# Sums of weights loaded into the tiles of x: six of the loads in each second half's pairs leave the ring `avc`

## The chip, the cores and the metric

The kernel runs on one core of a Trainium2 chip. The metric is the device time of one execution in microseconds (us). Before the change it is 2368.85 us, the median of three runs (2365.73, 2368.85 and 2370.08).

## What is computed

The reference is a trunk of two layers over `x` of 256 tokens by 2048 features, in float32. Each layer adds a token mixer (mLSTM in layer 0, HGRN2 in layer 1) and then a gated feed-forward part to `h`; a last RMSNorm closes it. The change touches the feed-forward part and the norms around it:

```python
def conv_glu(hn, w_up, conv_w, conv_b, w_down):
    u = hn @ w_up                                  # 2048 -> 2 x 5504
    a, v = jnp.split(u, 2, axis=-1)
    ...                                            # c: convolution of width 3 over the tokens of a
    return (jax.nn.gelu(c, approximate=False) * v) @ w_down   # 5504 -> 2048
...
    h = h + mix
    h = h + conv_glu(rmsnorm(h, norm_ffn_g[layer]), ...)
return rmsnorm(h, final_g)
```

## The kernel before, in words

**Streaming and splitting.** The weights come from HBM in the order in which PE (the matrix engine) uses them. SP, the engine that issues these DMAs, loads tiles `raw` of 128x2048 floats (`load_raw`, L135; in the up-projection L395), of which three exist. A piece of a `raw` is cast on ACT to a rounded high part `wh` (L147) and DVE subtracts this from the original to get the low part `wl` (L148). A product of two matrices is three matmuls: high by high, high by low, low by high. `x`, the normed input of a projection, is split in the same way into the tiles `xt0` to `xt15`, one for each k-tile of 128 features (`Norm.take`).

**The feed-forward part** of a layer has two halves. The first holds 22 of the 43 k-tiles of the middle dimension and the second 21. In a half the up-projection comes first, one chunk per k-tile, 64 matmuls on the 16 tiles of x (L357 and L361); what it gives goes through bias, convolution, gelu and the split in scratch tiles `avc` (L1195 to L1207) and ends in tiles `g`. Then come two *pairs* (`pair`, run by `squares_by_seven`, whose matmuls are L236): the down-projection from the half's k-tiles to two of the four column blocks of 512 each. Two k-tiles form a *couple* u; couple u with two column blocks is a 2x2 block product. The couples in `SEVEN` need seven products instead of eight, Strassen's way (21 matmuls instead of 24), with sums of activations (`sx`) and four sums of weights: T2 and T3 (128x1024 together), T4 and T1 (128x512 each).

**Where the sums of weights come from.** For the couples in `FLY`, DVE makes them on the spot (`combine`, L207). All others are *stored*: `prepare` makes them during earlier stages and writes them to a scratch `tscr` in DRAM (L635). In the pair, `raw(u)` in `split_squares` then issues three DMAs: the couple's weights without B12 (1536 columns, L135), T2, T3 and T4 in one DMA of 128x1536 into a tile `T` (L198), and T1 into the columns of `raw` that are left (L199). The tile `T` is a buffer of the ring `avc`, of which there are `TEMP` = 3, and which the up-projection's scratch `avc` uses too. So a load L198 waits until DVE and ACT have read the buffer that was filled three turns earlier.

**What sets the order.** The program is written as if it ran one thing after the other. A framework puts the instructions of each engine into an order by simulating the engines, and places a semaphore wait wherever a tile is read, written or used again. Each engine, SP included, works its list off strictly in order: an instruction that waits holds up all behind it. The DMAs of SP share eight semaphores in turn (DMAHW0 to DMAHW7), so that at most eight of them are under way.

**x's tiles.** The second half's last up chunk is the last reader of `xt0` to `xt15`. They stand empty during the two pairs of that half, until the next norm writes them (layer 0: the norm of the HGRN2 mixer, whose transposes are L434) or the final norm puts its gain into four of them (`FinalNorm.load`, tiles `fg`, and two tiles `fl` in `half`).

Of the kernel before, what the change touches and what calls it, by code (L numbers as in the profile page):

```python
# [8 lines left out]
F32 = mybir.dt.float32  # L9
F32R = mybir.dt.float32r  # L10
# [5 lines left out]
P = 128  # L16
T = 256
D = 2048
KT = D // P
# [31 lines left out]
FLY = (2,), (5,), (2,), ()  # L51
FIRST = 6
SPLIT = (0, 2, 5), (0, 2, 5)
END = 3
SCRATCH = 4096
SEVEN_MIX = (2, 4, 6)
# [10 lines left out]
def trunk_kernel(ctx, tc, xT, x_d, fg_d, pp_d, cst_d, w_gate, w_first, w_aq, w_ak, w_av, w_ao, w_aout, w_ao2,  # L67
                 w_bq, w_bv, w_bg, w_bout, w_bo2, w_up, w_d0, w_d1, w_d3, out, mscr, tscr):
    nc = tc.nc
    act, dve, pool, pe = nc.scalar, nc.vector, nc.gpsimd, nc.tensor  # L70

    keep = ctx.enter_context(tc.tile_pool(name="keep", bufs=1))
# [110 lines left out]
    def temporary(pool_, name):  # L183
        ff = pool_.name == "ff"
        return pool_.tile([P, 1536], F32, tag="avc" if ff else name, bufs=TEMP if ff else 2, name=name)

    def split_squares(ch, parts):

        units, raws, kept = (ch.nk + 1) // 2, {}, {}
        side.until(lambda: all(ch.waits))  # L190

        def raw(u):
            if u not in raws and u < units:
                n = 1536 if u in ch.stored else min(2048, 1024 * ch.nk - 2048 * u)
                raws[u] = load_raw(ch.src, 2048 * u, 2048 * u + n)
                if u in ch.stored:
                    kept[u] = temporary(ch.pool, "T")
                    nc.sync.dma_start(kept[u], ch.stored[u][:, 0:1536])  # L198
                    nc.sync.dma_start(raws[u][:, 1536:2048], ch.stored[u][:, 1536:2048])  # L199
            return raws.get(u)  # L200

        def combine(u):
            r, T = raw(u), temporary(ch.pool, "T")
            B11, B22, B21, B12 = (r[:, j * 512:(j + 1) * 512] for j in range(4))
            T2, T3, T4 = (T[:, j * 512:(j + 1) * 512] for j in range(3))
            for x, y, out in ((B12, B22, T3), (B12, B11, B12), (B22, B12, T2), (B21, T2, T4)):
                dve.tensor_tensor(out, x, y, ALU.subtract)  # L207
            kept[u] = T

        for u in range(units):  # L210
            r = raw(u)
            yield *parts(r[:, 0:1024], 1024, more=ch.pool), 1
            if u + 1 in ch.seven and u + 1 not in ch.stored:
                combine(u + 1)
            if u in ch.seven:
                yield *parts(kept[u][:, 0:1024], 1024, more=ch.pool), 1
            if 2 * u + 1 < ch.nk:
                yield *parts(r[:, 1024:2048], 1024, more=ch.pool), 1
            if u in ch.seven:
                yield *parts(kept[u][:, 1024:1536], 512, more=ch.pool), 1  # L220

    def banks():
        return [psm.tile([P, 512], F32, tag="mm", name="mm") for _ in range(2)]
# [1 line left out]
    def squares_by_seven(ch, fetch, ready):  # L225
# [48 lines left out]
        for u in range(units):  # L274
            if ch.last and u == units - END:
                ending(u)
# [121 lines left out]
    class Norm:  # L398

        def __init__(self, gname, goff):  # L400
            self.g, self.o = gname, goff
            self.xs, self.rc_, self.R_ = [None] * KT, None, None

        def take(self, k, src, g=None, *pin):
            self.xs[k] = keep.tile([P, 2 * T], F32R, tag=f"xt{k}", name=f"xt{k}")
            split(self.xs[k], src, col(self.g, self.o + k) if g is None else g, *pin)

        def squares(self, c, pin=lambda ins: ins):
# [67 lines left out]
    class FinalNorm:  # L476
# [4 lines left out]
            self.rc = small[:, 8:10]  # L481

        def load(self):
            self.g = [keep.tile([P, 512], F32, tag=f"xt{c}", name=f"fg{c}") for c in range(4)]
            for c in range(4):
                pool.dma_start(self.g[c], fg_d[:, c * 512:(c + 1) * 512].broadcast_to([P, 512]))

# [17 lines left out]
        def half(self, ps, t):  # L505
            side.drain()
            ss, rc = self.ss[:, t], self.rc[:, t:t + 1]
            dve.tensor_tensor(hm[:, t, 1024:1536], hm[:, t, 1024:1536], ps[0], ALU.add)
            square(hm[:, t, 1024:1536], ss[:, 2:3])
            dve.tensor_scalar(rc, ss[:, 2:3], 1.0 / D, rc, ALU.mult, ALU.add)  # L510
            last = keep.tile([P, 512], F32, tag=f"xt{4 + t}", name="fl")
            h = hm[:, t, 1536:2048]
            dve.tensor_tensor(h, h, ps[1], ALU.add)
            m = 256 if t else 512
            dve.scalar_tensor_tensor(last[:, 0:m], h[:, 0:m], 1.0 / D, h[:, 0:m], ALU.mult, ALU.mult, accum_out=ss[:, 3:4])
            dve.tensor_tensor(rc, rc, ss[:, 3:4], ALU.add)
# [58 lines left out]
    def pair(src, nk, c0, x, sums, norm, seven):  # L575
# [31 lines left out]

        ch = Chunk("st", src, nk, x, done)
        ch.mid, ch.seven, ch.sums = mid, seven, sums
        ch.stored, ch.waits, ch.pool, ch.ends, ch.rest = {}, (), None, False, False  # L610
        return ch

    def prepare(tiles, todo, first, period, finished, start, ahead):
# [561 lines left out]
    def ffn(layer, norm, nxt):  # L1175
# [40 lines left out]
        for part, (f0, nf) in enumerate(((0, FA), (FA, FB))):  # L1216
# [14 lines left out]
                                    fixed=part + i > 0))  # L1231
            def two(src, c0, norm, seven, fly, shares, GT=GT, SX=SX, nf=nf):
                ch = pair(src, nf, c0, lambda k: GT[k], lambda u: SX[u], norm, seven)
                ch.waits, left = [], [u for u in seven if u not in fly]
                for n, (todo, finished) in zip(shares, [early[layer]] + lists):
                    for u in left[:n]:
                        store(ch, src, u, todo)
                    if n:
                        ch.waits.append(finished)
                    left = left[n:]  # L1240
                assert not left
                pairs.append(ch)
                return ch
# [26 lines left out]
    c, close0 = ffn(0, n1, n2)  # L1270
    chunks += c
    c = hgrn(n2, n3)
    b = c[0].before
# [6 lines left out]
    c, close1 = ffn(1, n3, nf)  # L1280
# [102 lines left out]
```

## Time and profile before

| | |
|---|---|
| runs | 2365.73, 2368.85, 2370.08 us |
| the profiled execution, its own time | 2366.48 us |
| its span, first to last instruction | 2364.5 us |
| granted clock of PE | 0.999 |
| layer 0, second half: its first pair starts | 975.12 us |
| layer 1, second half: its first pair starts | 2250.33 us |

The profiled execution is one more run. Its span leaves out 2.0 us around the first and last instruction. PE is busy nearly throughout, so that a gap in its row is what counts; a DMA or another engine matters only where it makes PE wait. Engines are PE, DVE (vector), ACT (scalar), POOL and SP; L numbers are lines of the kernel before.

### The profile page before, as it was taken

Reading aid. Unit: us, or ns where it says so; the run is one execution under the profiler, and the core shown is the slowest. Engines: PE = TensorE matmul, PEld = TensorE weight load, DVE = VectorE, ACT = ScalarE, POOL = GpSimd, SP = SyncE. Lnnn points to the kernel's source line nnn. Section 1 sums busy time; section 2 is a strip of 40 time slices with the busy share of each in tenths; the row PEclk is TensorE's granted clock in tenths of the full one; section 3 lists DMA queues with packets and bytes.
Section 4 is the critical chain, followed back from the end, with each engine's and each line's share of the span. In section 5 each row is a group of like instructions: output and inputs, shape, how many; then the busy total and the mean of one; then the engine's idle time right before and its main releaser. Section 6 shows DMA issues by size and latency. Waiting matters only on the chain. (4 is left out here: it accounts for less than half of the span.)

```text
span 2364.5 us, 38407 instructions
## 1 busy us (share of the span) xinstructions
PE 2354.1 (100%) x14545; PEld 2016.2 (85%) x14545; DVE 1993.5 (84%) x3087; ACT 1470.0 (62%) x2340; POOL 196.5 (8%) x244
## 2 busy tenths in 40 slices
PE   9999999999999999999999999999999999999998
PEld 8888888888888888888888888888888888888887
DVE  7777687888998898897888888778789889888888
ACT  7655456555665555676777777776555567455565
POOL 0100000000000000000232322220000000000000
PEclk9999999999999999999999999999999999999999
DMA  8776656888888878996556665646788888888896
GB/s 303 239 248 242 213 195 211 295 282 292 313 321 327 306 282 292 330 334 230 208 203 223 212 225 204 214 169 228 270 300 289 289 321 335 295 287 302 309 351 221
DMA packets 122266, 632.97 MB, mean 268 GB/s; under 512 B 13776, under 2 KB 14928, under 8 KB 77664
## 3 DMA queue, kind: packets, MB, share of 16 engines
q1 hardware_dynamic: 120384, 626.51, 75.0%
q0 software_dynamic: 1120, 3.21, 0.8%
q8 instruction: 114, 1.87, 0.3%
q10 hardware_dynamic: 576, 0.79, 0.1%
q14 instruction: 72, 0.59, 0.1%
HBM read 562.24 MB, written 68.22 MB: 267 GB/s over the span
## 5 line engine op out<-in xcount | busy, mean ns | idle before, releaser
L357 PE MATMUL mm<-xt,wh 128*128 128x512 f32 x3776 | 1312.0, 394 | 0.0
L148 DVE TENSOR_TENSOR wl<-raw,wh 128x1024 fp32r<-128x1024 f32 (+1 forms) x844 | 1037.3, 1234 | 222.6 <-ACT wh L147 214.5
L147 ACT CAST wh<-raw 128x1024 fp32r<-128x1024 f32 (+1 forms) x844 | 875.3, 1042 | 513.0 <-PE mm L357 305.8
L361 PE MATMUL mm<-xt,wl 128*128 128x256 f32 x3776 | 1043.5, 278 | 0.0
L357 PEld LDWEIGHTS mm<-xt,wh 128*128 128x128 f32 x3776 | 705.6, 188 | 160.6 <-issue 0.4
L361 PEld LDWEIGHTS mm<-xt,wl 128*128 128x128 f32 x3776 | 709.4, 188 | 4.5
L373 PE MATMUL mm<-wh,xt 128*128 128x512 f32 x1024 | 324.4, 392 | 0.6 <-ACT wh L147 0.5
L236 PE MATMUL pc<-wh,g 128*128 128x512 f32 (+1 forms) x716 | 243.2, 388 | 0.3 <-ACT wh L147 0.2
L373 PEld LDWEIGHTS mm<-wh,xt 128*128 128x128 f32 x1024 | 191.2, 188 | 40.0 <-ACT wh L147 1.1
L632 DVE TENSOR_TENSOR praw<-praw 128x512 f32<-128x512 f32 x252 | 174.1, 691 | 44.7 <-DMA praw<-in_w_d 29.0
L373 PE MATMUL mm<-wl,xt 128*128 128x512 f32 x512 | 199.7, 391 | 0.0
L236 PEld LDWEIGHTS pc<-wh,g 128*128 128x128 f32 x716 | 134.1, 188 | 29.0 <-ACT wh L147 1.5
L236 PE MATMUL mm<-wh,sx 128*128 128x512 f32 x432 | 153.4, 389 | 0.0
L148 DVE TENSOR_TENSOR wl<-T,wh 128x1024 fp32r<-128x1024 f32 (+1 forms) x144 | 135.9, 955 | 13.3 <-ACT wh L147 8.9
L147 ACT CAST wh<-T 128x1024 fp32r<-128x1024 f32 (+1 forms) x144 | 118.6, 835 | 44.7 <-DMA T<-tscr 18.2
L236 PE MATMUL pc<-wl,g 128*128 128x512 f32 (+1 forms) x358 | 138.8, 388 | 0.0
L591 POOL TENSOR_TENSOR hm<-hm,u 128x512 f32<-128x512 f32 x10 | 14.8, 1481 | 1223.8 <-DVE u L590 1223.8
L373 PEld LDWEIGHTS mm<-wl,xt 128*128 128x128 f32 x512 | 96.2, 188 | 18.6
L1071 DVE TENSOR_TENSOR QK<-QK,G 128x256 f32<-128x256 f32 x224 | 104.6, 515 | 6.2 <-ACT kq L1050 5.9
L1195 ACT COPY avc<-mm 128x256 f32<-128x256 f32 x172 | 64.0, 372 | 63.9 <-PE mm L361 63.6
L1050 ACT COPY kq<-QK 128x512 f32<-128x512 f32 x112 | 74.5, 669 | 37.3 <-DVE QK L1071 29.5
L236 PEld LDWEIGHTS mm<-wh,sx 128*128 128x128 f32 x432 | 81.0, 188 | 16.9 <-ACT wh L147 0.2
(246 smaller groups left out, 2263.1 us busy)
## 6 DMA issues: line engine op xcount, KB each, us to landing
raw<-in_w_up SPq DMA_DIRECT2D x172, 1024.0 KB, 6.1
tscr<-praw SPq DMA_DIRECT2D x126, 512.0 KB, 6.7
praw<-in_w_d SPq DMA_DIRECT2D x120, 512.0 KB, 6.8
raw<-in_w_bq SPq DMA_DIRECT2D x48, 1024.0 KB, 5.0
T<-tscr SPq DMA_DIRECT2D x63, 768.0 KB, 7.6
raw<-in_w_d SPq DMA_DIRECT2D x60, 768.0 KB, 6.0
raw<-in_w_ao SPq DMA_DIRECT2D x24, 1024.0 KB, 4.8
raw<-in_w_d SPq DMA_DIRECT2D x24, 1024.0 KB, 7.7
```

Source lines behind the costliest of these rows:

```text
L147: pin(act.copy(wh[:, :m], r))
L148: pin(dve.tensor_tensor(wl[:, :m], r, wh[:, :m].bitcast(F32), ALU.subtract))
L236: pin(pe.matmul(ps, a, b, start=bank not in begun, stop=stop and i == 2))
L357: hold(pe.matmul(ps[f], wh[:, c:c + P], x, start=k + kk == 0, stop=False))
L361: hold(pe.matmul(ps[f][:, 0:T], wl[:, c:c + P], x[:, 0:T], start=False, stop=k + kk == ch.nk - 1))
L373: pe.matmul(ps[t], x[:, a + t * P:a + (t + 1) * P], w[:, c], start=st and i == 0, stop=sp and i == 2)
L591: pool.tensor_tensor(part(1, 0), part(1, 0), u, ALU.add)
L632: dve.tensor_tensor(out, x, y, ALU.subtract)
L1050: act.copy(m, blocks(QK, h))
L1071: dve.tensor_tensor(two[:, j], two[:, j], by[:, j], ALU.mult)
L1195: act.copy(z, p[:, T:2 * T])
```

## The change

`LENT` names three couples: 2, 3 and 4. In both pairs of a second half, in both layers, their T2 and T3 go into a whole tile of x (`xt3`, `xt5`, `xt6`) and their T4 into half of another (`xt4`, its other half, and half of `xt7`), instead of into a buffer of the ring `avc`. Since the place is in two tiles, the load is two DMAs, of 128x1024 and 128x512. For this the tiles of x now hold two k-tiles each: `xt0` to `xt7`, 128x1024 (in `before`, sixteen of half that size). The final norm's gain lies in the halves of `xt0` and `xt1`, and its scratch `fl` in the halves of `xt2`. All three couples are stored ones, in both layers.

```diff
+LENT = {2: (3, 4, 0), 3: (5, 4, 1), 4: (6, 7, 0)}
...
     def split_squares(ch, parts):
-        units, raws, kept = (ch.nk + 1) // 2, {}, {}
+        units, raws, kept, halves = (ch.nk + 1) // 2, {}, {}, {}
         side.until(lambda: all(ch.waits))
+
+        def place(u):
+            if u not in ch.lent:
+                T = temporary(ch.pool, "T")
+                return T[:, 0:1024], T[:, 1024:1536], T
+            i, j, h = ch.lent[u]
+            if j not in halves:
+                halves[j] = keep.tile([P, 1024], F32, tag=f"xt{j}", name="T")
+            return keep.tile([P, 1024], F32, tag=f"xt{i}", name="T"), halves[j][:, h * 512:(h + 1) * 512], None
...
                 if u in ch.stored:
-                    kept[u] = temporary(ch.pool, "T")
-                    nc.sync.dma_start(kept[u], ch.stored[u][:, 0:1536])
+                    kept[u] = place(u)
+                    for T, a, b in [(kept[u][2], 0, 1536)] if kept[u][2] else zip(kept[u], (0, 1024), (1024, 1536)):
+                        nc.sync.dma_start(T, ch.stored[u][:, a:b])
                     nc.sync.dma_start(raws[u][:, 1536:2048], ch.stored[u][:, 1536:2048])
...
-                yield *parts(kept[u][:, 0:1024], 1024, more=ch.pool), 1
+                yield *parts(kept[u][0], 1024, more=ch.pool), 1
...
-                yield *parts(kept[u][:, 1024:1536], 512, more=ch.pool), 1
+                yield *parts(kept[u][1], 512, more=ch.pool), 1
...
-            self.xs[k] = keep.tile([P, 2 * T], F32R, tag=f"xt{k}", name=f"xt{k}")
+            if k // 2 not in self.two:
+                self.two[k // 2] = keep.tile([P, 4 * T], F32R, tag=f"xt{k // 2}", name=f"xt{k // 2}")
+            self.xs[k] = self.two[k // 2][:, k % 2 * 2 * T:(k % 2 + 1) * 2 * T]
...
-            self.g = [keep.tile([P, 512], F32, tag=f"xt{c}", name=f"fg{c}") for c in range(4)]
+            g = [keep.tile([P, 1024], F32, tag=f"xt{c}", name=f"fg{c}") for c in range(3)]
+            self.g = [g[c // 2][:, c % 2 * 512:(c % 2 + 1) * 512] for c in range(4)]
+            self.last = g[2]
...
-            last = keep.tile([P, 512], F32, tag=f"xt{4 + t}", name="fl")
+            last = self.last[:, 512 * t:512 * t + 512]
...
                 ch = pair(src, nf, c0, lambda k: GT[k], lambda u: SX[u], norm, seven)
+                if part:
+                    ch.lent = LENT
```

The number of instructions on PE, DVE, ACT and POOL stays the same; SP issues 12 more, three in each of four pairs. Every engine's order and waits are the same in both kernels up to the last up chunks of layer 0's second half, and again from the HGRN2 mixer's first chunk to layer 1's second half. What is between differs.

**SP where layer 1's second half turns to its first pair.** Before: T_23012 is couple 1's T, raw_23107 to raw_23233 the weights of couples 2 to 5, and T_23109, T_23151 and T_23193 the T of couples 2 to 4.

```order
L198 DMA T_23012<-tscr 128x1536 [waits DMAHW7_49]
L135 DMA raw_23107<-in_w_d0 128x1536 [waits DMAHW0_49,DVE_49]
L199 DMA raw_23107<-tscr 128x512 [waits DMAHW1_49]
L135 DMA raw_23149<-in_w_d0 128x1536 [waits DMAHW2_49,DVE_49]
L199 DMA raw_23149<-tscr 128x512 [waits DMAHW3_49]
L135 DMA raw_23191<-in_w_d0 128x1536 [waits DMAHW5_49,DMAHW4_49,DVE_49]
L198 DMA T_23109<-tscr 128x1536 [waits DVE_49]
L199 DMA raw_23191<-tscr 128x512 [waits DMAHW6_49]
L198 DMA T_23151<-tscr 128x1536 [waits DMAHW7_49,DVE_49]
L198 DMA T_23193<-tscr 128x1536 [waits DMAHW0_49,DVE_49]
L135 DMA raw_23233<-in_w_d0 128x1536 [waits DMAHW1_49,DVE_49]
```

The changed kernel at the same place: T_22990 is couple 1's T; raw_23084, raw_23128 and raw_23171 are the weights of couples 2 to 4; T_23087 and T_23086 hold the two parts of couple 2's sums, and so on. The lines L209 and L210 are L198 and L199 of before.

```order
L209 DMA T_22990<-tscr 128x1536 [waits DMAHW5_49]
L136 DMA raw_23084<-in_w_d0 128x1536 [waits DMAHW6_49,DVE_49]
L210 DMA raw_23084<-tscr 128x512 [waits DMAHW7_49]
L209 DMA T_23087<-tscr 128x1024 [waits DMAHW0_49,PE_49]
L136 DMA raw_23128<-in_w_d0 128x1536 [waits DMAHW1_49,DVE_49]
L210 DMA raw_23128<-tscr 128x512 [waits DMAHW2_49]
L209 DMA T_23086<-tscr 128x512 [waits DMAHW3_49,PE_49]
L209 DMA T_23086<-tscr 128x512 [waits DMAHW4_49]
L209 DMA T_23130<-tscr 128x1024 [waits DMAHW5_49,PE_49]
L209 DMA T_23174<-tscr 128x1024 [waits DMAHW6_49,PE_49]
L209 DMA T_23173<-tscr 128x512 [waits DMAHW7_49,PE_49]
L136 DMA raw_23171<-in_w_d0 128x1536 [waits DMAHW0_49,DVE_49]
```

Couple 2's T2 and T3 now stand ahead of couple 3's weights, where they stood behind couple 4's, and wait for PE's last reading of a tile of x instead of for DVE. All six lent loads stand ahead of couple 4's weights.

**SP further on in the same pair.** Before: raw_23275, raw_23317 and raw_23359 are the weights of couples 6, 7 and 8, T_23235, T_23277 and T_23319 the T of couples 5 to 7, and T_23470 is the T of the second pair's couple 1.

```order
L135 DMA raw_23233<-in_w_d0 128x1536 [waits DMAHW1_49,DVE_49]
L199 DMA raw_23233<-tscr 128x512 [waits DMAHW2_49]
L198 DMA T_23235<-tscr 128x1536 [waits DMAHW5_49,DMAHW3_49,DVE_49]
L135 DMA raw_23275<-in_w_d0 128x1536 [waits DMAHW4_49,DVE_49]
L199 DMA raw_23275<-tscr 128x512
L198 DMA T_23277<-tscr 128x1536 [waits DMAHW7_49,DMAHW6_49,DVE_49]
L135 DMA raw_23317<-in_w_d0 128x1536 [waits DVE_49]
L199 DMA raw_23317<-tscr 128x512 [waits DMAHW0_49]
L198 DMA T_23319<-tscr 128x1536 [waits DMAHW1_49,DVE_49]
L135 DMA raw_23359<-in_w_d0 128x2048 [waits DMAHW2_49,DVE_49]
```

The changed kernel: raw_23215, raw_23257 and raw_23299 are the weights of couples 5, 6 and 7; T_23217, T_23259 and T_23301 are the T of couples 5 to 7; T_23537, T_23582 and T_23536 belong to couples 2 and 3 of the *second* pair.

```order
L209 DMA T_23217<-tscr 128x1536 [waits DMAHW2_49,DVE_49]
L209 DMA T_23259<-tscr 128x1536 [waits DMAHW3_49,DVE_49]
L209 DMA T_23537<-tscr 128x1024 [waits DMAHW4_49,DVE_49]
L136 DMA raw_23215<-in_w_d0 128x1536 [waits DMAHW5_49,DVE_49]
L210 DMA raw_23215<-tscr 128x512 [waits DMAHW6_49]
L209 DMA T_23301<-tscr 128x1536 [waits DMAHW7_49,DVE_49]
L209 DMA T_23582<-tscr 128x1024 [waits DMAHW0_49,DVE_49]
L209 DMA T_23536<-tscr 128x512 [waits DMAHW1_49,DVE_49]
L209 DMA T_23536<-tscr 128x512 [waits DMAHW2_49]
L136 DMA raw_23257<-in_w_d0 128x1536 [waits DMAHW3_49,DVE_49]
L210 DMA raw_23257<-tscr 128x512 [waits DMAHW4_49]
```

The second pair's lent loads are issued during the first pair, as soon as DVE has read the first pair's sums out of the tiles of x, and ahead of the first pair's couple 6. So are T6 (ahead of couple 5's weights) and T7 (ahead of couple 6's).

**ACT at couple 2 of the same pair.** Before: wh_23097 is from couple 1's T4; wh_23112 and wh_23132 are from couple 2's weights and wh_23122 from its T2 and T3; L1200 and L1203 belong to the last up chunk's convolution and gelu.

```order
L147 CAST wh_23097<-T_23012 128x512
L1195 COPY avc_23035<-mm_22931 128x256
L1200 ACTIVATE avc_23035<-avc_23035,pp_70 128x256
L1203 ACTIVATE avc_23035<-avc_23035 128x256
L147 CAST wh_23112<-raw_23107 128x1024
L1206 CAST g20_23046<-avc_23035 128x256
L147 CAST wh_23122<-T_23109 128x1024
L147 CAST wh_23132<-raw_23107 128x1024
```

The changed kernel, where wh_23101 is from couple 2's T2 and T3, and wh_23091 and wh_23111 from its weights (L1215 and L1218 are L1200 and L1203 of before).

```order
L148 CAST wh_23074<-T_22990 128x512
L1210 COPY avc_23013<-mm_22909 128x256
L1215 ACTIVATE avc_23013<-avc_23013,pp_70 128x256
L148 CAST wh_23101<-T_23087 128x1024
L1218 ACTIVATE avc_23013<-avc_23013 128x256
L148 CAST wh_23091<-raw_23084 128x1024
L148 CAST wh_23111<-raw_23084 128x1024
L1221 CAST g20_23024<-avc_23013 128x256
```

The cast of T2 and T3 has moved from behind the cast of the couple's weights to ahead of the gelu. On PE two matmuls with `wh` of T2 and T3 now come first in couple 2, ahead of the first two with the couple's weights; before, the couple's weights came first with all six of their matmuls.

More of the change, by code (lines that the diff above doesn't have):

```diff
@@ L202, in combine @@
         def combine(u):
-            r, T = raw(u), temporary(ch.pool, "T")
+            r, (T, T4, _) = raw(u), place(u)
             B11, B22, B21, B12 = (r[:, j * 512:(j + 1) * 512] for j in range(4))
-            T2, T3, T4 = (T[:, j * 512:(j + 1) * 512] for j in range(3))
+            T2, T3 = (T[:, j * 512:(j + 1) * 512] for j in range(2))
             for x, y, out in ((B12, B22, T3), (B12, B11, B12), (B22, B12, T2), (B21, T2, T4)):
                 dve.tensor_tensor(out, x, y, ALU.subtract)
-            kept[u] = T
+            kept[u] = T, T4
         for u in range(units):
@@ L401, in __init__ @@
             self.g, self.o = gname, goff
-            self.xs, self.rc_, self.R_ = [None] * KT, None, None
+            self.xs, self.two, self.rc_, self.R_ = [None] * KT, {}, None, None
         def take(self, k, src, g=None, *pin):
-            self.xs[k] = keep.tile([P, 2 * T], F32R, tag=f"xt{k}", name=f"xt{k}")
+            if k // 2 not in self.two:
+                self.two[k // 2] = keep.tile([P, 4 * T], F32R, tag=f"xt{k // 2}", name=f"xt{k // 2}")
+            self.xs[k] = self.two[k // 2][:, k % 2 * 2 * T:(k % 2 + 1) * 2 * T]
             split(self.xs[k], src, col(self.g, self.o + k) if g is None else g, *pin)
@@ L609, in pair @@
         ch.mid, ch.seven, ch.sums = mid, seven, sums
-        ch.stored, ch.waits, ch.pool, ch.ends, ch.rest = {}, (), None, False, False
+        ch.stored, ch.waits, ch.pool, ch.ends, ch.rest, ch.lent = {}, (), None, False, False, {}
         return ch
```

## The prediction

> **What bounds the kernel now.** I read the page's busy row first, then what PE waits for, then the PE row at each place that the change touches, and behind it ACT, DVE and the landings of the DMAs there.
>
> ```profile
> PE 2354.1 (100%) x14545; PEld 2016.2 (85%) x14545; DVE 1993.5 (84%) x3087; ACT 1470.0 (62%) x2340; POOL 196.5 (8%) x244
> ```
>
> PE is busy 2354.1 of 2364.5 us, and the change leaves its instructions as they are. So the sum is about gaps in PE's row, and there are few. The waits of PE, in all, the number of times and the longest, in us:
>
> ```profile
> PE idle L1266 <- POOL ones L1259: 1.1, 1, 1.1
> PE mm L236 <- DVE wl L148: 0.5, 1, 0.5
> PE mm L373 <- ACT wh L147: 0.5, 2, 0.3
> PE pc L236 <- ACT wh L147: 0.2, 1, 0.2
> ```
>
> The first row is the start of the program, the third the start of HGRN2 (L373 is its first product). Both waits of the pairs (L236) lie in layer 1's second half, in its first pair. PE's row there (start, duration):
>
> ```profile
> 2250.33 0.40 PE L236 MATMUL pc<-wh,g 128*128 128x512 f32 x1
> ...
> 2260.31 0.39 PE L236 MATMUL pc<-wh,g 128*128 128x512 f32 x1
> 2260.54 0.49 PE L236 MATMUL mm<-wh,g 128*128 128x512 f32 x1
> 2260.86 0.40 PE L236 MATMUL pc<-wh,g 128*128 128x512 f32 x1
> 2261.79 0.50 PE L236 MATMUL mm<-wl,g 128*128 128x512 f32 x1 [0.53 <-DVE wl L148]
> 2262.13 0.40 PE L236 MATMUL mm<-wh,g 128*128 128x512 f32 x1
> ...
> 2263.39 0.50 PE L236 MATMUL pc<-wh,g 128*128 128x512 f32 x1
> 2263.73 0.39 PE L236 MATMUL mm<-wh,sx 128*128 128x512 f32 x1
> ```
>
> From the pair's first matmul (2250.33) to couple 2's first (2260.54) lie couple 0's 24 matmuls and couple 1's 21: 10.21 / 45 = 0.227 us each, the undisturbed pace. From 2260.31 to 2263.73 PE takes ten steps, which would be 2.27 us, and needs 3.42. **The stall at couple 2 costs 1.15 us**, in three gaps. Its causes stand on ACT, and behind ACT on a DMA:
>
> ```profile
> 2259.12 0.42 ACT L1203 ACTIVATE avc<-avc 128x256 f32<-128x256 f32 x1 [1.13 <-DVE avc L1202]
> 2259.44 1.03 ACT L147 CAST wh<-raw 128x1024 fp32r<-128x1024 f32 x1
> ...
> 2261.34 1.05 ACT L147 CAST wh<-T 128x1024 fp32r<-128x1024 f32 x1 [0.56 <-DMA T<-tscr]
> ```
>
> The cast of couple 2's weights stands behind the last gelu, for which ACT sat idle 1.13 us, and ends at 2260.47, just when PE wants it; DVE's subtraction behind it is what PE waits 0.53 us for. The cast of T2 and T3 then waits 0.56 us for its DMA, and the next cast of weights behind it is the gap at 2263.39. That DMA was issued late, since the ring `avc` was full:
>
> ```profile
> L198 SPq DMA_DIRECT2D T<-tscr x1: 432/432/432, 2255.4 to 2255.4; - x1
> DMA to landing us min/median/max: 5.9/5.9/5.9
> ```
>
> It was issued at 2255.4 and landed at 2261.3.
>
> **The change part by part. 1: the stall at couple 2 goes, −1.1 us.** T2 and T3 now wait for PE's last reading of `xt3` (k-tiles 6 and 7). The last up chunk, and what stands ahead of the load on SP, couple 2's weights:
>
> ```profile
> 2239.00:2250.00 11.00, 11.00 (x66) 9.61 (x65) 9.11 (x14) 6.16 (x10) 2.21 (x4) 1.00 0.96 340
> 2242.16 0.33 SPq L135 DMA_DIRECT2D raw<-in_w_d  x1
> L135 SPq DMA_DIRECT2D raw<-in_w_d x1: 333/333/333, 2247.1 to 2247.1; - x1
> DMA to landing us min/median/max: 9.2/9.2/9.2
> ```
>
> The chunk's matmuls take 11.00 / 66 = 0.167 us, and 32 of its 64 come behind k-tile 7, so this is read 5.3 us before 2250.33, at 2245.0. The load starts ten microseconds earlier than before. By the list it goes out just ahead of couple 3's weights, which landed at 2256.3; with its 0.52 MB more (1.2 us at 0.42 MB per us, part 4) and their 0.79 less (1.9 us) it lands at about 2255.6. Its cast stands ahead of the gelu in ACT's list, where ACT was idle 1.13 us, and takes 1.05: it is hidden there, ends by 2259.1, and gives PE two matmuls (0.45 us) that it now does first. The weights' low part was ready when the matmul at 2261.79 began, and now isn't wanted before 2260.54 plus seven or more steps, 2262.1. So none of the three gaps has a cause left, and what is late next is couple 3's weights, which had no gap. The price if the load landed after 2258 is up to the whole of it: 0 to −1.15, and I take −1.1.
>
> **2: the ring's other loads come earlier,** since three buffers less are asked of it in each pair: T5, T6 and T7 are not late in either kernel (no row of PE waits for them). Nothing.
>
> **3: twelve more DMAs.** A load becomes two. What a DMA of 256 KB costs in a full queue is shown by neighbours, the T1 of couples 3 and 7 (L199) and T7 (L198):
>
> ```profile
> L199 SPq DMA_DIRECT2D raw<-tscr x1: 424/424/424, 2247.5 to 2247.5; - x1
> DMA to landing us min/median/max: 9.5/9.5/9.5
> ...
> L199 SPq DMA_DIRECT2D raw<-tscr x1: 414/414/414, 2273.2 to 2273.2; - x1
> DMA to landing us min/median/max: 7.0/7.0/7.0
> L198 SPq DMA_DIRECT2D T<-tscr x1: 319/319/319, 2274.6 to 2274.6; - x1
> DMA to landing us min/median/max: 7.6/7.6/7.6
> ```
>
> Couple 3's T1 landed at 2257.0, 0.7 us behind its weights (2256.3, above); T7's 0.79 MB landed at 2282.2, 2.0 us behind T1 of couple 7 at 2280.2. That is time by bytes, some 0.4 MB per us, with no visible fixed part: a load cut in two costs the queue nothing. The issue costs SP 0.4 us more, and SP has nothing else to do but wait. I take 0; the upper bound is rival D.
>
> The Trainium skill, "DMA: Bandwidth & Descriptors", speaks against the cut: it wants DMAs of 1 MiB or more, and its section "Anatomy of one DMA — SWDGE (gpsimd) path" fits a DMA's time as 2.0 us and bytes by 436 GB/s. By that, as serial time, 12 more DMAs would be an estimated 24 us; the rows above show no such step between neighbours on this queue, where landings overlap.
>
> **4: arrears in the first pair, +0.5 us.** Now the bytes. Pair two's lent loads are issued in pair one, ahead of couple 6's weights, and so are T6 and T7. DMAs are not idle there:
>
> ```profile
> 2275.00:2280.00 5.00, 5.00 (x24) 4.14 (x23) 4.91 (x6) 4.10 (x5) 0.00 (x0) 1.00 1.02 415
> ...
> 2255.00:2260.00 5.00, 5.00 (x24) 4.14 (x23) 3.71 (x9) 1.48 (x3) 0.00 (x0) 1.00 0.82 291
> 2260.00:2265.00 5.00, 4.47 (x19) 2.93 (x18) 4.14 (x5) 4.44 (x7) 0.00 (x0) 1.00 0.98 354
> 2265.00:2270.00 5.00, 5.00 (x24) 4.14 (x23) 5.00 (x6) 5.00 (x6) 0.00 (x0) 1.00 0.90 317
> ```
>
> The last two columns are the share of the DMA engines and GB/s: full is 1.02 at 0.42 MB per us, and before 2275 some is free. From 2257.0, when couple 3's weights had landed, up to the first 1536 columns of couple 6's weights, the changed list holds 9.17 MB: the six lent loads 2.36, weights of 4, 5 and 6 with two T1 2.88, T5 to T7 2.36, and 1.57 of the second pair's. At 0.42 that lands at 2278.9. Before, it was
>
> ```profile
> L135 SPq DMA_DIRECT2D raw<-in_w_d x1: 333/333/333, 2267.7 to 2267.7; - x1
> DMA to landing us min/median/max: 6.8/6.8/6.8
> ```
>
> 2274.5. PE reaches couple 6 after 24 + 5 x 21 = 129 matmuls, at 2250.33 + 129 x 0.227 = 2279.6; with the cast's 1.05 the weights are ready at 2280.0. So PE is late by 0.4, and I take +0.5. Bounds: nothing, if a part of the lent loads went out before 2257.0, as the list allows for T2 and T3 (0.52 MB, 1.2 us); and +3.5, if none of the additional 3.14 MB (7.5 us) finds free time, so that landing falls 7.5 us behind 2274.5, of which 4.0 are in hand. Couples 7 and 8 come after the same bytes and lose no more.
>
> In **layer 0** the same list moves, with more in hand:
>
> ```profile
> L135 SPq DMA_DIRECT2D raw<-in_w_d x1: 332/332/332, 1001.9 to 1001.9; - x1
> DMA to landing us min/median/max: 5.5/5.5/5.5
> 1008.67 0.39 PE L236 MATMUL mm<-wh,g 128*128 128x512 f32 x1
> 975.00:1000.00 25.00, 25.00 (x112) 20.73 (x111) 22.89 (x30) 18.02 (x25) 0.00 (x0) 1.00 0.88 305
> ```
>
> The weights for the matmul at 1008.67 (couple 7) were loaded at 1001.9 in a pair whose first 25 us use 0.88 of the DMAs: the 0.12 left over is 3 us, or 1.3 MB, and the buffers of `raw` give about 5.9 us of lead. 2.88 MB more ahead are 6.9 us, less the lead 1.0 late at most, less the free time nothing. I take 0, bounds 0 and +1.0. The second pairs then have fewer bytes to load; PE waits for nothing in them before, so nothing is won.
>
> **5: the start of HGRN2.** The five transposes with which the next norm begins write the tiles of x, now two k-tiles to a tile, and are grouped otherwise (runs of 4, 8 and so on). The row of waits has 0.5 us there. A writer must now wait for both halves' readers; those are done long before. I take 0, bounds −0.7 (that wait and the switches gone) and +0.5 (one such wait more).
>
> **Sum:** −1.1 + 0 + 0.5 + 0 + 0 = −0.6 us on the profiled execution's 2366.48, 2365.9. That execution lies 2.4 us below the median of the runs, within their spread of 4.4 us (2365.73 to 2370.08); on the median's scale the time is 2368.85 − 0.6, about **2368.3**.
>
> **The rivals.** *A, slower: arrears in the DMA queue.* The mechanism is part 4 at its bounds: the second pair's sums are fetched 25 us before they are needed, ahead of couple 6's weights. It decides when those land after 2278.5, one cast ahead of PE. For it: shares of 1.02 from 2275 on, and a sum that already passes this point by 0.4 us. Against it: free shares of 2 to 18% before 2270. Its price is up to 3.5 + 1.0 − 1.1 = +3.4, that is 2372.3. *B, the stall goes and nothing replaces it,* with the HGRN2 bound: −1.1 − 0.7 = −1.8, 2367.0. The lead of 4.0 us speaks for it. *C, the change doesn't do what it says:* another wait on couple 2 (the gelu stays ahead of its weights' cast) takes the gap's place, 2368.8. Against it: only the cast of T2 must be early for PE to have work. *D, a DMA has a fixed price on the queue.* Its price is in a load of 0.79 MB in layer 0's pair, the quickest there:
>
> ```profile
> L135 SPq DMA_DIRECT2D raw<-in_w_d x1: 333/333/333, 997.9 to 997.9; - x1
> DMA to landing us min/median/max: 4.3/4.3/4.3
> ```
>
> Of the 4.3 us 1.9 are bytes at 0.42; 12 x 2.4 = 29 us, 2397. The 0.7 us between neighbours speak against it.
>
> **How the numbers follow.** Forecast 0.52, A 0.24, B 0.13, C 0.09, D 0.02. A measurement of this kernel tells about 0.2% (4.7 us) from no change, so most cases are "within". The range goes from B less half the spread of the runs (2.2), 2364.9, to A plus the same, 2374.5. Faster by over 0.2% (below 2364.1) is B with a low draw: 0.03. Slower (above 2373.6) is D, and A where its bounds don't hold, which I give half of A: 0.14. Within: 0.83.
>
> **What would show it.** Right: in layer 1's first pair the load of T2 and T3 issues near 2245, the rows at couple 2 keep a pace of 0.227, and "PE mm L236 <- DVE wl" is gone. Part 4 shows as a wait of PE on a cast of couple 6's weights whose ACT row names the DMA `raw<-in_w_d`; as a landing before 2278 it is wrong. In layer 0 no new wait should stand between 1000 and 1027. The forecast is wrong if PE's waits in the pairs sum to over 3 us, if the second pairs have any, or if the granted clock changes.

## The result, and the profile after

The changed kernel takes 2371.4 us (median of 22 runs, 2368.64 to 2374.48), the kernel before on the same chip 2367.82 us (22 runs, 2365.26 to 2370.44). The ratio is 1.0016, with a 95% interval from 1.0009 to 1.0022: **slower by 3.6 us**, from 2.1 to 5.2. The forecast was 0.6 us faster; rival A, arrears in the DMA queue, had said up to 3.4 us slower.

The profiled execution of the changed kernel took 2368.64 us (span 2366.7), 2.2 more than that of before. Busy row of the page and PE's waits after (L247 is L236 of before, L384 is L373, L148 and L149 are L147 and L148):

```profile
PE 2355.3 (100%) x14545; PEld 2016.4 (85%) x14545; DVE 1995.3 (84%) x3087; ACT 1470.2 (62%) x2340; POOL 195.4 (8%) x244
```

```profile
PE idle L1283 <- POOL ones L1276: 1.1, 1, 1.1
PE pc L247 <- DVE wl L149: 0.8, 2, 0.4
PE mm L384 <- ACT wh L148: 0.6, 1, 0.6
PE mm L247 <- ACT wh L148: 0.5, 2, 0.3
```

The wait of couple 2 on DVE is gone, as part 1 had it; four other waits of the pairs stand in its place, three in layer 1's first pair and one, of 0.41 us, in layer 0's. (L384's lies at the start of the program, at 9.5 us.) First couple 2 of layer 1's first pair, which begins at 2250.87 here. Its load of T2 and T3, then ACT's rows, then PE's:

```profile
L209 SPq DMA_DIRECT2D T<-tscr x1: 320/320/320, 2245.5 to 2245.5; - x1
DMA to landing us min/median/max: 10.1/10.1/10.1
```

```profile
2256.82 1.04 ACT L148 CAST wh<-T 128x1024 fp32r<-128x1024 f32 x1
2258.05 0.42 ACT L1218 ACTIVATE avc<-avc 128x256 f32<-128x256 f32 x1 [0.19 <-DVE avc L1217]
2258.37 1.98 ACT L148 CAST wh<-raw 128x1024 fp32r<-128x1024 f32 x2
```

```profile
2261.08 0.62 PE L247 MATMUL mm<-wh,sx 128*128 128x512 f32 x2
2261.54 0.39 PE L247 MATMUL mm<-wh,g 128*128 128x512 f32 x1
2261.76 0.39 PE L247 MATMUL pc<-wh,g 128*128 128x512 f32 x1
2261.99 0.39 PE L247 MATMUL mm<-wl,sx 128*128 128x512 f32 x1
```

The load is issued at 2245.5 and lands at 2255.6; part 1 had 2245.0 and 2255.6, for a pair that began 0.5 us earlier. Its cast lies in the gap ahead of the gelu (0.19 us of idle time left of 1.13), and PE goes on at 0.227 us a step. Further on in the same pair stand couple 6 (from 2280.55) and couples 8 and 9 (from 2291.45, within the group of five matmuls at 2290.47, which takes 1.71 us where four steps and a matmul are 1.30):

```profile
2279.90 0.39 PE L247 MATMUL mm<-wh,sx 128*128 128x512 f32 x1
2280.55 0.50 PE L247 MATMUL mm<-wh,g 128*128 128x512 f32 x1 [0.26 <-ACT wh L148]
2280.89 0.40 PE L247 MATMUL pc<-wh,g 128*128 128x512 f32 x1
2281.50 0.73 PE L247 MATMUL mm<-wh,sx 128*128 128x512 f32 x2 [0.22 <-ACT wh L148]
...
2290.47 1.71 PE L247 MATMUL pc<-wh,g 128*128 128x512 f32 x5
2292.60 0.50 PE L247 MATMUL pc<-wl,g 128*128 128x512 f32 x1 [0.42 <-DVE wl L149]
...
2294.34 0.50 PE L247 MATMUL pc<-wl,g 128*128 128x512 f32 x1
```

The weights for them, couple 6's first 1536 columns and couple 8's (2048), and the DMA share of the stretch (last columns: share, GB/s):

```profile
L136 SPq DMA_DIRECT2D raw<-in_w_d x1: 333/333/333, 2269.2 to 2269.2; - x1
DMA to landing us min/median/max: 10.2/10.2/10.2
L136 SPq DMA_DIRECT2D raw<-in_w_d x1: 333/333/333, 2277.5 to 2277.5; - x1
DMA to landing us min/median/max: 11.4/11.4/11.4
```

```profile
2255.00:2260.00 5.00, 5.00 (x24) 4.14 (x23) 4.26 (x8) 3.50 (x5) 0.00 (x0) 1.00 1.04 401
2265.00:2270.00 5.00, 5.00 (x24) 4.14 (x23) 5.00 (x6) 4.59 (x6) 0.00 (x0) 1.00 1.01 406
2275.00:2280.00 5.00, 5.00 (x24) 4.04 (x22) 1.78 (x2) 1.33 (x2) 0.00 (x0) 1.00 1.03 405
2290.00:2295.00 5.00, 4.39 (x17) 2.67 (x16) 4.97 (x8) 3.01 (x4) 0.00 (x0) 1.00 0.91 373
```

From 2250 to 2290 the queue is full (shares of 1.01 to 1.05), where before 2 to 18% were free until 2270. Couple 6's weights land at 2279.4, couple 8's at 2288.9. From 2275 to 2280 ACT is busy for 1.33 us and DVE for 1.78: they have little left that has landed, and PE follows. The cast of couple 6's weights in this trace, and in a second trace of the changed kernel that is described below:

```profile
2279.45 1.05 ACT L148 CAST wh<-raw 128x1024 fp32r<-128x1024 f32 x1 [3.67 <-PE pc L247]
```

```profile
2280.82 1.04 ACT L148 CAST wh<-raw 128x1024 fp32r<-128x1024 f32 x1 [4.55 <-DMA raw<-in_w_d]
```

The first row names PE and not the DMA, against the sign that the prediction gave; the second names the DMA. In both the cast starts 0.1 us behind the landing (2279.4 and 2280.7), so it is the landing that I hold for the cause.

A measure that carries over from trace to trace is the length of layer 1's last two pairs, from the first to the last of their 477 matmuls. Without any gap it is 104.88 us; the excess over this is in the table, with the places at which it arises (0.3 us with layer 1 alone lie behind couple 9) and the landings counted from the pair's start. Due is couple 6's landing at 28.2 (129 x 0.227, less the cast's 1.05) and couple 8's at 37.8 (171 x 0.227, less 1.05).

| kernel | excess, us | at couple 2 | at couple 6 | at couples 8 and 9 | couple 6 lands | couple 8 lands |
|---|---|---|---|---|---|---|
| before | 1.10 | all | 0 | 0 | 24.2 | 34.3 |
| before, second trace | 1.63 | all | 0 | 0 | 25.5 | 35.0 |
| changed | 2.48 | 0 | 1.03 | 1.44 | 28.5 | 38.0 |
| changed, second trace | 4.55 | 0.52 | 2.52 | 1.46 | 30.5 | 40.1 |
| layer 1 alone lent | 3.16 | 0.26 | 2.60 | 0 | 30.3 | 39.9 |
| couple 4 of the second pairs held | 2.87 | 0.70 | 2.16 | 0 | 30.3 | 37.9 |
| second pairs held | 0.00 | 0 | 0 | 0 | 25.6 | 33.2 |
| first pairs alone lent | 0.01 | 0 | 0 | 0 | 26.3 | 33.9 |

### The profile page after: what moved, and what is told of

Its sections match the earlier page's. It is cut to its first block, busy times and chain, and to the rows that moved or that the text cites. A ratio compares the mean times of both kernels' runs of the same rounds, so it can differ in the third digit from the quotient of the medians.

```text
span 2366.7 us, 38412 instructions
## 1 busy us (share of the span) xinstructions
PE 2355.3 (100%) x14545; PEld 2016.4 (85%) x14545; DVE 1995.3 (84%) x3087; ACT 1470.2 (62%) x2340; POOL 195.4 (8%) x244
## 5 line engine op out<-in xcount | busy, mean ns | idle before, releaser
L149 DVE TENSOR_TENSOR wl<-raw,wh 128x1024 fp32r<-128x1024 f32 (+1 forms) x844 | 1037.3, 1235 | 237.9 <-ACT wh L148 229.8
L148 ACT CAST wh<-raw 128x1024 fp32r<-128x1024 f32 (+1 forms) x844 | 875.3, 1043 | 540.1 <-PE mm L368 323.7
L384 PE MATMUL mm<-wh,xt 128*128 128x512 f32 x1024 | 324.4, 393 | 0.6 <-ACT wh L148 0.6
L247 PE MATMUL pc<-wh,g 128*128 128x512 f32 (+1 forms) x716 | 243.2, 388 | 0.2
L384 PEld LDWEIGHTS mm<-wh,xt 128*128 128x128 f32 x1024 | 191.6, 188 | 40.1 <-ACT wh L148 1.2
L384 PE MATMUL mm<-wl,xt 128*128 128x512 f32 x512 | 199.8, 391 | 0.0
L247 PEld LDWEIGHTS pc<-wh,g 128*128 128x128 f32 x716 | 134.0, 188 | 28.4 <-ACT wh L148 1.0
L247 PE MATMUL mm<-wh,sx 128*128 128x512 f32 x432 | 152.4, 389 | 0.2 <-ACT wh L148 0.2
L149 DVE TENSOR_TENSOR wl<-T,wh 128x1024 fp32r<-128x1024 f32 (+1 forms) x144 | 135.4, 956 | 12.7 <-ACT wh L148 12.3
L148 ACT CAST wh<-T 128x1024 fp32r<-128x1024 f32 (+1 forms) x144 | 117.9, 834 | 40.4 <-DMA T<-tscr 15.1
L247 PE MATMUL pc<-wl,g 128*128 128x512 f32 (+1 forms) x358 | 139.1, 389 | 0.9 <-DVE wl L149 0.8
L384 PEld LDWEIGHTS mm<-wl,xt 128*128 128x128 f32 x512 | 96.2, 188 | 18.6
L247 PEld LDWEIGHTS mm<-wh,sx 128*128 128x128 f32 x432 | 81.0, 188 | 17.4 <-ACT wh L148 0.7
```

Source lines behind the costliest of these rows:

```text
L148: pin(act.copy(wh[:, :m], r))
L149: pin(dve.tensor_tensor(wl[:, :m], r, wh[:, :m].bitcast(F32), ALU.subtract))
L247: pin(pe.matmul(ps, a, b, start=bank not in begun, stop=stop and i == 2))
L384: pe.matmul(ps[t], x[:, a + t * P:a + (t + 1) * P], w[:, c], start=st and i == 0, stop=sp and i == 2)
```

## The experiments

The theory was arrears: the second pair's sums go out in the first pair, ahead of weights that are needed 25 us before them. The rivals were a price for the twelve more DMAs, and one for the tiles of two k-tiles. Each ratio is against runs of the kernel before that were taken together with the experiment (medians of 2367.67 for the first four, 2367.84 for the next three, 2368.07 for the last three).

**Second pairs' lent loads held back.** A pinned load stays behind all that is written ahead of it on SP; the rest of SP's list is unchanged. On ACT, DVE and PE the order in layer 1's pair is that of the changed kernel up to the end of couple 6, here and in every experiment below that lends couples 2 to 4 to both pairs of layer 1 or to both first pairs; behind it, and in layer 0, the orders differ in places.

```diff
-                        nc.sync.dma_start(T, ch.stored[u][:, a:b])
+                        (late if ch.held and u in ch.lent else nc.sync.dma_start)(T, ch.stored[u][:, a:b])
...
                     ch.lent = LENT
+                    ch.held = c0 > 0
```

> The changed kernel, but the second pairs' lent loads are pinned behind all loads that are written ahead of them, so that they are issued in the second pair and not in the first. Theory (arrears: the second pairs' sums, fetched 25 us early, push the first pairs' weights of couples 6 to 9 back): the waits of PE in both first pairs go (2.5 us in layer 1, 0.7 in layer 0 in the changed kernel's profile), and the stall at couple 2 stays away; about 3 us below the changed kernel, 1 to 2 us below the kernel before. Rival 1 (twelve more DMAs have a price of their own): as the changed kernel, 3.6 us above before. Rival 2 (x's tiles of two k-tiles cost something wherever x is written): also as the changed kernel.

Measured: 2365.77 us (11 runs) against 2367.67 (33 runs of before); ratio 0.9991, 0.9982 to 1.0000. PE's waits, and couple 6's and couple 8's weights:

```profile
PE mm L384 <- ACT wh L148: 1.1, 2, 0.9
PE pc L247 <- ACT wh L148: 0.2, 1, 0.2
PE mm L247 <- ACT wh L148: 0.2, 1, 0.2
```

```profile
L136 SPq DMA_DIRECT2D raw<-in_w_d x1: 333/333/333, 2269.2 to 2269.2; - x1
DMA to landing us min/median/max: 8.1/8.1/8.1
...
L136 SPq DMA_DIRECT2D raw<-in_w_d x1: 333/333/333, 2277.9 to 2277.9; - x1
DMA to landing us min/median/max: 7.0/7.0/7.0
```

From issue to landing couple 6's weights take 2.1 us less than in the changed kernel's first trace, couple 8's 4.4 less. Against the pair's start (2251.69 here) they land 2.9 and 4.8 us sooner than in that trace, and 4.9 and 6.9 sooner than in its second. The bytes that are no longer ahead of them, 1.57 and 2.36 MB, are 3.7 and 5.6 us at 0.42 MB per us. Neither last pair has a gap (the two waits of L247 left lie in another stage, near 1932, and L384's at the start of the program). All twelve more DMAs and all tiles of x are as in the changed kernel, so neither rival has a share that can be seen: the whole loss goes by moving six loads in each layer. By the two ratios this kernel is some 6 us faster than the changed one, twice the 3 us expected.

**The layout of x's tiles alone.**

```diff
-LENT = {2: (3, 4, 0), 3: (5, 4, 1), 4: (6, 7, 0)}
+LENT = {}
```

> The changed kernel with an empty LENT: tiles of x with two k-tiles each and the final norm's tiles in them, but every sum in the ring as before. Theory (arrears): as before within 0.7 us, the stall of 1.15 us at couple 2 of layer 1's first pair back, no wait in the rest of the pairs; if the 0.7 us that the changed kernel's profile has less at the start of HGRN2 belongs to the layout, they are gone here too. Rival 1: as before. Rival 2: up to 3.6 us above before, and the stretches in which x is written (start of the program, of HGRN2, of the up-projections) longer than before.

Measured: 2367.76 us, ratio 1.0001 (0.9992 to 1.0010). The stall at couple 2 is there (excess 1.56 us). No cost of the layout can be seen. The stretch with the start of HGRN2, from the last matmul of layer 0's pairs to the first of layer 1's, takes 1170.7 us in this trace as in the first one of before, so what the changed kernel's first trace has less there (0.6 us by this measure) isn't the layout's.

**The loads cut in two, in the ring.**

```diff
-                    nc.sync.dma_start(kept[u], ch.stored[u][:, 0:1536])
+                    for a, b in ((0, 1024), (1024, 1536)) if ch.cut and u in (2, 3, 4) else ((0, 1536),):
+                        nc.sync.dma_start(kept[u][:, a:b], ch.stored[u][:, a:b])
```

> The kernel before, in which the loads of T2 to T4 of couples 2, 3 and 4 of the second halves' pairs are cut in two DMAs of 128x1024 and 128x512 into the same buffer of the ring: twelve more DMAs, nothing else. Theory (arrears): as before within 0.5 us, the stall at couple 2 as before or a few tenths shorter, since T2 and T3 land before T4. Rival 1: 3.6 us above before. Rival 2: as before.

Measured: 2367.88 us, ratio 0.9998 (0.9989 to 1.0007). No cost of twelve more DMAs can be seen (rival D's 29 us are far outside). Its trace has no stall at couple 2 (excess 0.01): couple 1's T landed 0.8 us earlier than in the first trace of before, with the same order on ACT, and the last gelu and the casts behind it came earlier by as much.

**Lent in the first pairs alone.**

```diff
-                if part:
+                if part and c0 == 0:
```

> The changed kernel with LENT in the first pair of each second half alone. Theory (arrears): no sums of the second pair ahead of the first pair's weights, so no arrears: no wait in the pairs, 1 to 2 us below before, like the kernel that holds the second pairs' loads. Rival 1 (price per DMA): half of the 3.6 us, 1.8 above before. Rival 2 (layout): as the changed kernel, 3.6 above before.

Measured: 2365.43 us, ratio 0.9988 (0.9979 to 0.9997): 2.2 us below before. Its interval is clear of no change; that of the kernel that holds the second pairs' loads just reaches it, and the two can't be told apart. Its trace has no gap in the pairs.

**Only couple 4 of the second pairs held.** This is the dose: 0.79 MB fewer ahead of couple 8, the rest early.

```diff
-                        (late if ch.held and u in ch.lent else nc.sync.dma_start)(T, ch.stored[u][:, a:b])
+                        (late if ch.held and u == 4 else nc.sync.dma_start)(T, ch.stored[u][:, a:b])
```

> The changed kernel with only couple 4's lent loads of the second pairs (0.79 MB) held back to the second pair; those of couples 2 and 3 stay early. Theory (arrears, a matter of bytes ahead): the weights of couples 8 and 9 land 1.9 us earlier than in the changed kernel, so the gaps there (1.34 us in layer 1, 0.69 at couple 9 in layer 0) go, while those at couple 6 of layer 1 (1.03 us) stay; 1.5 to 2 us below the changed kernel, 1.5 to 2 above before. Rival (SP's order or its semaphores hold the loads, not the bytes): the gaps stay where they are or go all together.

Measured: 2369.32 us, ratio 1.0006 (0.9997 to 1.0015), 1.5 us above before by the medians and not clear of it. PE's rows at couple 6, at couples 8 and 9, and at the start of layer 0's second pair:

```profile
2282.58 0.50 PE L247 MATMUL mm<-wh,g 128*128 128x512 f32 x1 [1.39 <-ACT wh L148]
...
2292.55 1.29 PE L247 MATMUL pc<-wh,g 128*128 128x512 f32 x5
2293.68 0.39 PE L247 MATMUL pc<-wl,g 128*128 128x512 f32 x1
...
1028.69 0.50 PE L247 MATMUL mm<-wh,sx 128*128 128x512 f32 x1 [0.22 <-ACT wh L148]
1029.33 0.50 PE L247 MATMUL mm<-wl,g 128*128 128x512 f32 x1
```

From couple 6's landing to couple 8's it is 7.6 us here and 9.5 and 9.6 in the changed kernel: 1.9 us less, which is the 0.79 MB, as bytes ahead have it. The gap at couple 6 stays, and 0.70 us of the stall at couple 2 with it; those at couples 8 and 9 are gone. These last can't be put to the bytes alone, since ACT's order at couple 8 differs here as well (see the experiment with layer 1 alone). New are gaps of 1.4 us together at the start of layer 0's second pair, which no one had expected; their cause was not followed up.

**Lent in the second pairs alone.**

```diff
-                if part:
+                if part and c0 == 2:
```

> The changed kernel with LENT in the second pair of each second half alone: the first pair's sums all go through the ring as before, and the second pair's 2.36 MB are issued before the first pair's T2, because the tiles of x are free then. Theory (arrears): T2 and T3 of couple 2 land about 5 us later than in the kernel before, PE waits 4 to 6 us at couple 2 of layer 1's first pair; 3 to 8 us above before, more than the changed kernel, which has twice as many lent loads. Rival (price per lent load): half of the changed kernel's, 1.8 us above before.

Measured: 2374.87 us (6 runs), ratio 1.0030 (1.0018 to 1.0042), 7 us above before with half of the lent loads. PE's longest wait, and the windows around it (the column ahead of the DMA share is PE's granted clock):

```profile
PE mm L247 <- ACT wh L148: 5.9, 1, 5.9
```

```profile
2262.00:2268.00 6.00, 0.10 (x2) 0.05 (x1) 0.07 (x1) 1.15 (x2) 0.00 (x0) 0.95 0.99 403
2268.00:2274.00 6.00, 6.00 (x14) 4.49 (x15) 6.00 (x6) 4.73 (x6) 0.00 (x0) 0.50 0.58 194
2274.00:2276.00 2.00, 2.00 (x9) 1.60 (x9) 1.19 (x3) 1.38 (x2) 0.00 (x0) 0.95 0.87 322
```

ACT's row for the cast of couple 2's T2 and T3:

```profile
2266.85 1.04 ACT L148 CAST wh<-T 128x1024 fp32r<-128x1024 f32 x1 [7.04 <-DMA T<-tscr]
```

The tiles of x are free at the pair's start, so the whole 2.36 MB go ahead of T2 and T3. These land at 2266.8, 16.5 us behind the pair's start where it was 11.0 before, and PE waits 5.9 us at couple 2.

**Both kernels once more.**

> The changed kernel once more, for a second trace. Theory: 3.6 us above before; waits at couples 6, 8 and 9 of layer 1's first pair, 1.5 to 4.5 us together, and less than 1.5 us in layer 0's. If the waits differ from the first trace by a us or so, that is how far one trace can be from the median.

> The kernel before once more, for a second trace. If the stall at couple 2 is the same in every run, 1.15 us again; if it hangs on when couple 1's T lands, which differs from run to run (in the kernel with loads cut in two it landed 0.8 us earlier and there was no stall), anything between 0 and 1.6 us.

Measured: the changed kernel 2371.29 us, ratio 1.0016 (1.0007 to 1.0025), the same as in the first result; one run of the kernel before, 2366.30. Waits of PE on the pairs' casts, of the changed kernel's second trace and then of the other:

```profile
PE mm L247 <- ACT wh L148: 2.2, 3, 1.8
...
PE pc L247 <- DVE wl L149: 0.8, 2, 0.4
```

```profile
PE mm L236 <- DVE wl L148: 0.5, 1, 0.5
PE mm L236 <- ACT wh L147: 0.4, 1, 0.4
```

The excess is 4.55 and 1.63 us, where the first traces had 2.48 and 1.10. Both the stall that the change removes and the arrears that it makes differ by a us or two from run to run. The two traces of the changed kernel already differ where the pair begins: couple 1's T lands 0.4 us ahead of its start in the first and 2.1 us behind it in the second.

**One layer at a time, and one pair.**

```diff
-                if part:
+                if part and layer == 1:
```

with `layer == 0` in the second and `layer == 1 and c0 == 0` in the third.

> The changed kernel with LENT in layer 1 alone. Theory (arrears): layer 1's first pair takes the waits at couples 6, 8 and 9 (2.5 and 4.5 us in two traces of the changed kernel) for the stall at couple 2 (1.05 and 1.6 in two traces of the kernel before), so 1 to 3.5 us above before, likeliest 2.3; no gap at couple 9 of layer 0. Rival (the cost lies in layer 0 or in the norms between): within 0.7 us of before.

> The changed kernel with LENT in layer 0 alone. Theory (arrears): the gap at couple 9 of layer 0's first pair (0.69 us in both traces) and nothing won, since no stall stood in layer 0; 0.3 to 1.3 us above before, and the stall at couple 2 of layer 1 as before. Rival: most of the 3.6 us.

> The changed kernel with LENT in layer 1's first pair alone, the only pair in which PE waited before. Theory: the whole gain of lending is here, 1.0 to 1.6 us below before, and no arrears; the kernel with both first pairs lent (2.2 below) is no better than this one within what the runs can tell.

Measured: layer 1 alone 2369.25 us, ratio 1.0003 (0.9995 to 1.0012); layer 0 alone 2367.88, 0.9996 (0.9987 to 1.0005); the one pair 2367.40, 0.9994 (0.9985 to 1.0003), against 2368.07 of before. Layer 1 alone shows the gap at couple 6 (2.60 of the excess of 3.16), but none at couples 8 and 9, though couple 8's weights land as late as in the changed kernel's second trace. ACT's rows there, first of that trace, then with layer 1 alone (L599 belongs to `mid`, which empties the seven products' sums behind couple 7):

```profile
2290.32 0.58 ACT L599 COPY u<-mm 128x512 f32<-128x512 f32 x1 [2.67 <-PE mm L247]
2290.80 2.00 ACT L148 CAST wh<-raw 128x1024 fp32r<-128x1024 f32 x2
```

```profile
2290.43 2.00 ACT L148 CAST wh<-raw 128x1024 fp32r<-128x1024 f32 x2 [2.72 <-DMA raw<-in_w_d]
2292.34 0.58 ACT L599 COPY u<-mm 128x512 f32<-128x512 f32 x1
```

With layer 1 alone the casts stand ahead of the copy that waits for PE, as they do in both traces of before; PE's own order at couples 8 and 9 is the same in both kernels. Couple 8's weights land equally late, 1.8 us before PE reaches couple 8, in this trace and in both of the changed kernel. So a landing as late doesn't make the 1.4 us at couples 8 and 9; it takes the changed kernel's order on ACT, in which the casts wait behind a copy that waits for PE. Whether that order would make them with an early landing too, no run shows. The gap at couple 9 of layer 0 is there with layer 0 alone (0.7 us in its trace) and gone with layer 1 alone, as expected, but the times of the two kernels can't be told from before, nor does their sum reach the changed kernel's 3.6 us by the medians; within the intervals it can. The kernel with one pair lent has no gap in layer 1 (excess 0.00). In its trace there is a wait of 1.9 us in layer 0, where SP's list and the engines' orders are those of the kernel with the layout alone, which doesn't have it:

```profile
1028.94 0.47 PE L247 MATMUL pc<-wh,g 128*128 128x512 f32 x1 [1.90 <-DVE hm L613]
```

DVE came late there because the weights that it splits just before landed 47.7 us behind the pair's start, where it is 45.6 in the layout kernel's trace, and its two subtractions took 4.26 us, with POOL at work beside them, where they took 3.45. Why this execution's loads landed later isn't settled, and so neither is whether that kernel is worse than the one with both first pairs lent.

## Why the prediction was wrong

- **Part 1 (stall at couple 2, −1.1) was right in its mechanism, and its size was read from one execution.** Issue, landing and the place of the cast were as worked out, and without the arrears the stall is gone (the kernels with the second pairs held or not lent). With them three of four traces keep 0.26 to 0.70 us of it. In the five traces of kernels that load all of layer 1's sums through the ring the excess is 1.10, 1.63, 1.56, 0.01 and 1.96 us, 1.25 in the mean. It goes with a landing that part 1 didn't name, that of couple 1's T, whose cast stands ahead of the last gelu on ACT: 1.2, 1.6, 1.7 and 1.9 us behind the pair's start go with 1.10, 1.56, 1.63 and 1.96, and 0.2 with 0.01. With the sums lent the same landing costs less: nothing at 0.6 to 1.2 us, 0.26 at 1.8, 0.70 at 2.2.
- **Two rows of PE's waits were put in the wrong place.** The 0.5 us of L373 lie in the program's first 10 us (0.22 at 5.6 and 0.29 at 9.0), not at the start of HGRN2, and the 0.2 us of `pc L236` lie at 1931.3, not in layer 1's second half. Part 5's bounds and rival B's price hang on the first of them.
- **Parts 2 and 3 (other ring loads, twelve DMAs: 0) were right.** The Trainium skill, "DMA: Bandwidth & Descriptors", section "Bandwidth", has the rule to batch DMAs to 1 MiB or more. For this cut, of 0.79 MB into 0.52 and 0.26, no run shows a cost: the kernel with the loads cut in two lies between 0.11% below and 0.07% above before.
- **Part 4 is the step that failed: it had the mechanism, and +0.5 us where the arrears cost 2.5, 4.0 and 2.9** (layer 1's excess without couple 2's share, in the changed kernel's two traces and with layer 1 alone). Two things in it were wrong.
- **First, couple 6 was sized at its best case.** The landing was forecast at 2278.9 − 2250.33 = 28.6 us behind the pair's start and came at 28.5 in the first trace and at 30.3 to 30.5 in three others, so that the agreement with the first is in part luck. The gap is then 0.5 to 2.1 us, and the next cast, which comes behind the late one, adds another 0.5. I had put "+0.5" where the working gave 0 to +3.5 and already stood past the deciding point.
- **Second, "couples 7 and 8 come after the same bytes and lose no more".** The bytes are the same: from couple 2's weights up to couple 6's SP loads 7.34 MB before and 10.49 in the changed kernel, up to couple 8's 11.27 and 14.42, which is 3.15 more in both. But they do lose more. Couple 8's own lead was not worked out (3.5 us by the due time of 37.8, where couple 6 had 4.0, and its landing moved by 3.7), nor where its casts stand on ACT: in the changed kernel they come behind the copy that waits for PE. Couples 8 and 9 lose 1.44 and 1.46 us there.
- **Layer 0 was put at 0 within bounds of 0 and +1.0, and loses 0.7 us at couple 9,** in one of three traces another 0.3 in the second pair. The working had the lead of couple 7's weights alone. Couple 9's land 41.0 us behind the pair's start before and 43.0 in the changed kernel. The order on ACT has a part here too: in the three traces with this gap the copy stands ahead of couple 8's casts, and in two others, in which couple 9's weights land as late (42.8 and 43.2) and the copy stands behind them, there is none.
- **Part 5 (start of HGRN2, 0) can't be told from right.** The stretch between the pairs of the two layers takes 1170.7 and 1170.1 us in the two traces of before and 1170.0 and 1169.5 in the changed kernel's, within the bounds.
- **The sum.** The mean excess of the three traces with layer 1 lent is 3.40, against 1.25 without: +2.15 in place of −0.6. With +0.8 in layer 0 this is 2.9 of the 3.6 us measured, within its interval (2.1 to 5.2). Rival A had the mechanism, its place and the deciding point; it should have been the forecast, since the sum had passed the point at which it decides. That its price of 3.4 comes so near is partly luck: it is made of couple 6 at its upper bound of 3.5, where couple 6 costs 2.0 in the mean, and has nothing for couples 8 and 9.

## What to carry to other kernels

A buffer that comes free early lets the loads into it go out early, and on a full queue that is time taken from whatever is needed sooner: for each such load, set the bytes that are now ahead of every later load against that load's own lead, not only against the first one's, and look at what its cast stands behind. To win the early load without the arrears, hold it in place (here: pin the second pair's loads, or lend the first pair's alone), and the loss of 3.6 us becomes a gain of about 2. When a working lands at the point where a rival decides, the bounds and not the point are the forecast.

## What the runs showed of the hardware that was not expected

After PE's wait of 5.9 us in the kernel with the second pairs lent, its granted clock is 0.50 for another 6 us (the windows above: 14 matmuls in 6.00 us, 0.43 us each, against 0.227), and with it the wait costs 9.08 us of excess in place of 5.9. Waits of up to 1.9 us in the other traces have left the clock at 1.00. The Trainium skill, "TensorE: Matmul & The Clock Gate", Part 1: The HAM clock gate (the "warmup" mystery), says that PE's clock falls to half after at least one idle window of some 3.4 us and returns after at least one busy one, and that these windows run on without regard to the kernel. This trace agrees: the clock is 0.50 from 2267.4 to 2274.2, which is two such windows, and PE stood idle for the first 0.6 us of them.
